# The second attention of a two-layer trunk: scores of a unit adjacent in three PSUM banks under one masked minimum, queries and keys transposed unsplit, norms of two tiles at once

## The chip, the cores and the metric

One core of a Trainium2 chip runs the whole program. The time is the device's, in microseconds (us), from one launch; the figure compared is the median of three runs. On the core, TensorE (PE in the profile, its weight loads PEld) multiplies and transposes, VectorE (DVE), ScalarE (ACT) and GpSimd (POOL) work on tiles, and SyncE (SP) issues the transfers. Each engine executes its own list of instructions in order and waits on semaphores for the others.

## The reference, cut to what matters

The program is a trunk of two layers over 1024 latent tokens of width 1024, with 256 context tokens beside them. Layer 0 has a two-dimensional neighbourhood attention and a gated convolutional feed-forward network; layer 1 has a sliding-window attention and another such network. The change is in the attention of layer 1: 16 query heads of 64 in 4 groups, each group with one key and one value head, a window of 128 to either side, all 256 context keys, and one sink logit per head.

```python
def attn_inputs(h, w_qkv, g_q, g_k, n_kv, with_q=True):
    y = h @ w_qkv
    q = rmsnorm(y[..., :D_MODEL].reshape(bsz, t, n_kv, N_HEADS // n_kv, HEAD_DIM), g_q)
    k = rmsnorm(kv[..., :kv_w].reshape(bsz, t, n_kv, HEAD_DIM), g_k)
...
def attend(q, k, v, bias=None, mask=None, sink=None):
    s = jnp.einsum('...qngd,...knd->...ngqk', q, k).astype(jnp.float32) * (HEAD_DIM ** -0.5)
    s = jnp.where(mask, s, NEG_INF)
    s = jnp.concatenate([s, sink_col], axis=-1)
    p = jax.nn.softmax(s, axis=-1)
    p = p[..., :-1]
...
    def block_step(j):          # 8 blocks of 128 queries
        valid = band & ((kpos >= 0) & (kpos < seq))[None, :]
        mask = jnp.concatenate([valid, ctx_ok], axis=-1)
        return attend(q_j, jnp.concatenate([k_j, k_c], axis=1), jnp.concatenate([v_j, v_c], axis=1),
                      mask=mask, sink=sink)
```

## The kernel before

All arithmetic is in 32 bits. Where a matmul needs the full precision, an operand is kept as two parts in the format that the source calls F32R: a rounded high part ("hi") and the rest ("lo"), and the products of the parts are added in PSUM. A plain F32 tile can be transposed on TensorE as it is.

**Order of the work.** Every stage is planned before it is written out: a scheduler (`Sched`) is given operations with an engine, an estimated cost, a key that says how early each is wanted, what it reads and writes, and which buffers it takes (`acq`) and gives back (`rel`); it lists them engine by engine, and that list is what the engines execute. A table `KINDS` shifts the keys of a kind of operation, a table `RANKS` those of single operations. All instructions are issued by one helper, so that the profile shows them all at line L51; they are told apart by the names of their tiles.

**The stage of the second attention** holds, in one list: the keys and values of the context (`plan_ctx_kv`); 32 tiles of query, key and value (`plan_sw_qkv`: 8 blocks of 128 tokens by 4 groups, each 256 query columns, 64 of key, 64 of value); 64 units of attention (`plan_sw_su` and `plan_su`: a unit is 2 heads of one group for one block of queries); and the output projection (`plan_oproj1`), of which the first half is made inside the stage. Units start behind the tiles that they need (LEAD1 = 7.5 in their keys), so that most of the stage has projection matmuls (`mm`), turns (`pt`), scores (`s`) and products with the values (`pv`) interleaved on PE; when the projection matmuls are used up, matmuls of the output projection (`mm<-o0hi,whi` and its two companions) stand between the last units.

**A tile of query and key** (`plan_sw_qkv`, L2964): ACT copies 384 columns from PSUM (`qraw`); `plan_rstd` (L894) squares 320 of them into `qsq` (ACT), sums per head (DVE, `qv`), takes the power of minus one half on POOL (`qy`) and improves it on DVE by small operations on five columns (one for the mean with epsilon, three of a Newton step); `qn`, `qa`, `qb` and their sum are the scaled and rotated queries and key. ACT then writes the hi parts (`st`, 128x256 for queries and 128x128 for the key, doubled) and POOL or DVE the lo parts (`st`, `klt`). PE turns them: `trk`, one 128x128 transpose of the key's hi and one of its lo, and `trq`, four of the queries' hi and lo side by side. ACT copies the results from PSUM (`kkl`, `kll`, `q`).

**A unit** (`plan_su`, L945): `qkc` makes the context scores of both heads into one bank (four matmuls `s<-ckc,q` of 256 columns), `qkl` the latent scores of each head into a bank of its own (`s<-kkl,q` and `s<-kll,q`, 384 columns, 256 for the first and last block). There are three banks of the tag `s`, taken in turn. For each head DVE copies the context scores to `S` with their sign turned and takes the minimum with the sink (`ctx_part`, `S<-s,sink`); a second pass over the latent scores adds the mask `bandt` and goes on with that minimum (`lat_part`, `S<-s,bandt,m`). Both passes return it through an accumulator, which is read by an instruction of its own. POOL writes the sink's column (`S<-sink`). ACT exponentiates 641 (or 513) columns with that minimum as bias and sums them. PE turns `S` in groups of four 128x128 transposes, two in the last group (`pt<-idr,S`); ACT rounds a group to `pthi`, DVE subtracts for `ptlo`, PE multiplies both with the values (`pv<-pthi,vc`, `pv<-ptlo,vc` for the context, `,v` for latent tokens). Five buffers of `S`, two each of `pthi`, `ptlo` and of the bank tags `pt` and `mm`, one bank `pv`.

`plan_na_qkv`, the same step of the first attention, already takes two tiles at once: one sum over 128x520 and one power over eight columns. It is not part of the change but for the size of three small tiles.

Of the kernel before, what the change touches and what calls it, by code (L numbers as in the profile page):

```python
# [11 lines left out]
F32 = mybir.dt.float32  # L12
F32R = mybir.dt.float32r
AF = mybir.ActivationFunctionType
ALU = mybir.AluOpType
# [23 lines left out]
class InOrder:  # L39
# [7 lines left out]
    def __getattr__(self, name):  # L47
        f = getattr(self.eng, name)

        def call(*a, **k):  # L50
# [16 lines left out]
    sw=dict(cp=0.8, sq=-0.2, red=0.1, newton=-11.7, qn=1.5, qa=4.2, kd=-0.8, ev=9.9, mp=4, v=-2.6, dg=-7.4, bc=9.7,  # L67
          mul=0.4, hif=4.7, lof=0.4, mm=0.2, pw=-0.2, f=-1.5, qb=-0.4, qs=-8.3, qhi=-1.7, trk=-0.9, kev=6.2, lev=-1.5,
          trq=-5.5, qev=0.2, lat_part=-1.4, exp=0.5, lo=-0.2, pvm=0.1, up=-0.4, add=-0.2, rec=-9.6),
# [297 lines left out]
    sw={2: -6.6, 8: -6, 9: -2.2, 13: -4.8, 15: -17.2, 17: -3.9, 24: 6.7, 40: -31.3, 42: 2.4, 50: -2.6, 53: -0.8,  # L367
# [227 lines left out]
def trunk_kernel(ctx, tc, xperm, xtok, xseq, cc, wmod0, wmod, bmod, gnorm, na_wqkv, na_gq, na_gk, na_bias, na_wo,  # L595
# [281 lines left out]
    def plan_qkv_mm(sc, key, psa, h, tt, slabs, s, J, c0=0, hkey=None):  # L877
# [3 lines left out]
        for kt in range(KT):  # L881
            def mm(e, kt=kt):
# [3 lines left out]
                for i, (a, w) in enumerate(((hh, wh), (hl, wh), (hh, wl))):  # L886
# [7 lines left out]
    def plan_rstd(sc, key, J, c0, nh, wk, nsq, fold=None):  # L894

        I = J["id"]

# [15 lines left out]
        def mean(e):  # L913
            v = J["ms"][:, :nh]
            dve.tensor_scalar(out=v, in0=v, scalar1=1.0 / DH, scalar2=EPS, op0=ALU.mult, op1=ALU.add)
# [2454 lines left out]
```

## Time and profile before

| | before |
|---|---|
| median of three runs | 2733.84 us (2731.42 to 2735.31) |
| the profiled execution | 2736.26 us |
| its span (first to last instruction) | 2734.5 us |
| stage of the second attention on PE | 1619.1 to 2047.76 us of the span |
| mean granted TensorE clock | 0.997 of full speed |

The profile is of one execution. Its first part gives the busy time of each engine and its share of the span; then views of the trace give stretches of time (busy time of each engine in each), waits (which engine waited, for whom, in total and how often), groups of equal instructions (busy time, mean of one, idle time of the engine before them and who ended it), and single instructions with their start. Starts and durations of matmuls overlap, since they are pipelined: what one costs PE is the distance to the next start. The stage above runs from the first matmul of the context keys to the first of the output projection's second half.

### The profile page before, as it was taken

Reading aid. Unit: us, or ns where it says so; the run is one execution under the profiler, and the core shown is the slowest. Engines: PE = TensorE matmul, PEld = TensorE weight load, DVE = VectorE, ACT = ScalarE, POOL = GpSimd, SP = SyncE. Lnnn points to the kernel's source line nnn. Section 1 sums busy time; section 2 is a strip of 40 time slices with the busy share of each in tenths; the row PEclk is TensorE's granted clock in tenths of the full one; section 3 lists DMA queues with packets and bytes.
Section 4 is the critical chain, followed back from the end, with each engine's and each line's share of the span. In section 5 each row is a group of like instructions: output and inputs, shape, how many; then the busy total and the mean of one; then the engine's idle time right before and its main releaser. Section 6 shows DMA issues by size and latency. Waiting matters only on the chain.

```text
span 2734.5 us, 43669 instructions
## 1 busy us (share of the span) xinstructions
PE 2700.5 (99%) x15375; PEld 2382.1 (87%) x15375; DVE 2249.7 (82%) x4573; ACT 1665.5 (61%) x3198; POOL 437.2 (16%) x726
## 2 busy tenths in 40 slices
PE   7999999999999999999999999999999999999999
PEld 6999998998799987788888889999988888888887
DVE  5787787789689687899997799888987989888766
ACT  6777676778456554545555458888864655545443
POOL 1222333323000000000010016556430000000000
PEclk9999999999999999999999999999999999999999
DMA  7233333334656644454476561010263234334745
GB/s 288 82 102 105 112 115 101 112 112 141 235 161 186 185 166 135 154 169 135 162 246 220 178 224 33 19 35 19 85 205 123 74 115 154 116 116 144 260 149 190
DMA packets 153104, 387.29 MB, mean 142 GB/s; under 512 B 23356, under 2 KB 38708, under 8 KB 151476
## 3 DMA queue, kind: packets, MB, share of 16 engines
q1 hardware_dynamic: 152884, 384.50, 43.0%
q8 instruction: 121, 1.98, 0.3%
q14 instruction: 99, 0.81, 0.1%
HBM read 313.39 MB, written 71.04 MB: 141 GB/s over the span
## 4 chain that ended last, share of the span: by engine, by line
PE 73%; DVE 2%; ACT 1%; issue 0%; DMA 0%; POOL 0%; SPq 0%; DVEq 0%; ACTq 0%
PE ua L51 17%; PE dn L51 15%; PE uc L51 13%; PE mm L51 7%; PE oacc L51 5%; PE ud L51 4%; PE pt L51 3%; PE pv L51 3%; PE s L51 3%; PE dnc L51 2%; PE u L51 2%; PE mod L51 0%; DVE wlo L51 0%; DVE S L51 0%; DVE o0lo L51 0%
## 5 line engine op out<-in xcount | busy, mean ns | idle before, releaser
L51 ACT ACTIVATE whi<-wraw 128x512 fp32r<-128x512 f32 (+1 forms) x264 | 212.8, 808 | 181.5 <-PE uc L51 53.3
L51 DVE TENSOR_TENSOR wlo<-wraw,whi 128x512 fp32r<-128x512 f32 (+1 forms) x264 | 240.0, 911 | 40.3 <-ACT whi L51 39.9
L51 ACT ACTIVATE S<-S,m 128x640 f32<-128x640 f32 (+3 forms) x288 | 220.6, 767 | 36.7 <-DVE m L51 30.7
L51 ACT ACTIVATE pthi<-pt 128x512 fp32r<-128x512 f32 (+2 forms) x384 | 195.7, 522 | 76.2 <-PE pt L51 37.3
L51 PE MATMUL dn<-ghi,whi 128*128 128x512 f32 x616 | 239.9, 390 | 0.0
L51 PE MATMUL dn<-ghi,wlo 128*128 128x512 f32 x616 | 239.7, 389 | 0.0
L51 PE MATMUL dn<-glo,whi 128*128 128x512 f32 x616 | 239.6, 389 | 0.0
L51 DVE SCALAR_TENSOR_TENSOR u<-c,cv,u 128x1023 f32<-128x1023 f32 x176 | 222.1, 1279 | 3.3 <-ACT u L51 2.8
L51 ACT ACTIVATE whi<-s 128x1024 fp32r<-128x1024 f32 (+1 forms) x116 | 109.1, 940 | 165.0 <-PE uc L51 108.7
L51 ACT ACTIVATE ghi<-graw 128x512 fp32r<-128x512 f32 x154 | 96.4, 630 | 174.6 <-PE dn L51 99.5
L51 PE MATMUL pt<-idr,S 128*128 128x128 f32 x1280 | 194.5, 273 | 1.7 <-DVE pthi L51 1.3
L51 PE MATMUL mm<-whi,h0hi 128*128 128x384 f32 x480 | 168.8, 352 | 0.2 <-ACT qraw L51 0.2
L51 PEld LDWEIGHTS pt<-idr,S 128*128 128x128 f32 x1280 | 152.3, 140 | 16.7 <-DVE pthi L51 3.5
L51 DVE TENSOR_TENSOR glo<-graw,ghi 128x512 fp32r<-128x512 f32 x154 | 105.3, 688 | 71.6 <-ACT ghi L51 65.7
L51 PE MATMUL mm<-wlo,h0hi 128*128 128x384 f32 x480 | 161.5, 336 | 0.0
L51 POOL TENSOR_TENSOR n1y<-n1v,mhalf 128x4 f32<-128x4 f32 (+1 forms) x8 | 9.5, 1182 | 914.9 <-DVE n1v L51 914.9
L51 PE MATMUL pv<-pthi,v 128*128 128x256 f32 (+1 forms) x560 | 151.9, 353 | 3.4 <-DVE pthi L51 3.3
L51 DVE TENSOR_TENSOR pthi<-pt,pthi 128x512 fp32r<-128x512 f32 (+2 forms) x208 | 118.8, 582 | 35.6 <-ACT pthi L51 33.8
L51 DVE TENSOR_TENSOR wlo<-s,whi 128x1024 fp32r<-128x1024 f32 (+1 forms) x116 | 124.3, 1074 | 22.9 <-ACT whi L51 22.6
L51 PEld LDWEIGHTS dn<-ghi,wlo 128*128 128x128 f32 x616 | 115.6, 188 | 24.2
L51 PEld LDWEIGHTS dn<-glo,whi 128*128 128x128 f32 x616 | 115.6, 188 | 23.9
L51 PEld LDWEIGHTS dn<-ghi,whi 128*128 128x128 f32 x616 | 115.6, 188 | 23.7
(410 smaller groups left out, 8642.5 us busy)
## 6 DMA issues: line engine op xcount, KB each, us to landing
wraw<-in_w_up_dram SPq DMA_DIRECT2D x132, 512.0 KB, 3.9
wm<-in_wmod_dram SPq DMA_DIRECT2D x80, 512.0 KB, 4.0
wraw<-in_w_down_dram SPq DMA_DIRECT2D x44, 512.0 KB, 3.6
graw<-g_dram SPq DMA_DIRECT2D x44, 512.0 KB, 4.3
wraw<-in_w_down_dram SPq DMA_DIRECT2D x88, 256.0 KB, 3.1
graw<-g_dram SPq DMA_DIRECT2D x66, 256.0 KB, 2.7
slab<-in_na_wqkv_dram SPq DMA_DIRECT2D x32, 384.0 KB, 4.0
woraw<-in_na_wo_dram SPq DMA_DIRECT2D x24, 512.0 KB, 4.2
```

What stands on the lines that cost most here:

```text
L51: r = f(*a, **k)
```

## The change

Five things change, all in the stage of the second attention.

1. **Scores.** One tile `s3` of 1536 columns (three banks) takes the place of the three rotating banks. The scores of a head lie adjacent in it: the first head has its latent scores in bank 0 and its context scores at the start of bank 1, the second head its context scores at the end of bank 1 or at the start of bank 2. Written out, bank 0 holds the latent scores of one head, bank 1 the context scores of both, bank 2 the latent scores of the other; the middle bank is given back when both heads' minima have read it, the outer ones after one. The scores' matmuls are the same in number and size; they are issued bank by bank.
2. **One masked minimum.** Per head a single pass over 640 columns (512 for the first and last block) adds the mask and takes the minimum, starting from the sink. The mask tile has 7·128 columns, with zeros to either side of the band for the context scores; it lies in this stage's pool, so its load now stands behind the first weight slabs of this stage, and POOL writes the zeros. The sink's column is written first of all into `S`, so POOL now takes the buffer of `S`.
3. **Queries and keys turned unsplit.** The rotated F32 tiles `qa` of two blocks are turned as they are: four transposes for the queries and two for the keys per pair. ACT rounds the turned result from PSUM to the hi parts (`q`, twice 64x512; `kkl`, 128x256), and DVE subtracts for the lo parts (`q`, twice 64x512; `kll`, 128x256). The copies to `st` and `klt` are gone.
4. **Norms of two tiles at once.** Squares of two tiles go into one tile with a column of epsilon per head; one sum of 10 heads, one power of 10 columns, three small operations of 10 columns. The factor of the mean goes into the scale of the gains. The context keys are normed in the same way.
5. **Buffers and tables.** Four buffers of `qraw` for three, four of `qa` for two, a ring of four pairs of `q` for eight tiles; `KINDS` and `RANKS` of the stage are written anew, so that the list is another throughout.

```diff
+    s3 = ps.tile([P, 1536], F32, name="s3", tag="s3", bufs=1)
+    bandt = fin.tile([P, 7 * P], F32, name="bandt")
+    sc = Sched(dict(CAPS, qraw=4, s0=1, s1=1, s2=1, sqs=1, xl=4, qa=4, q=4), {"raw"})
+    sc.op("dma", 1.4, lambda e: dma.dma_start(bandt[:, 2 * P:5 * P], band), writes=[("band",)], key=-205)
...
     sw={2: -6.6, 8: -6, 9: -2.2, 13: -4.8, 15: -17.2, 17: -3.9, 24: 6.7, 40: -31.3, 42: 2.4, 50: -2.6, 53: -0.8,
...
+            for b in sorted(banks):
+                def qkb(e, b=b):
+                    for k, x, w in banks[b]:
...
+                        for i in range(2):
+                            pe.matmul(s3[:, c:c + w], u["q"], u[x][i], start=(i == 0), stop=(i == 1), skip_group_check=True)
+                sc.op("pe", sum(2 * t_pe(w) for _, _, w in banks[b]), qkb, reads=reads, writes=[K("s", b)], key=key,
+                      acq=[(f"s{b}", K("s", b), len({k for k, _, _ in banks[b]}))], rel=[rel] * len(banks[b]))
...
+                    pool.tensor_copy(J["S", k][:, n:n + 1], units[k]["get"]()["sink"])
+                sc.op("pool", 0.13, sink_part, reads=reads, writes=[K("Ss", k)], key=key - 0.5, acq=[("S", K("S", k), uses[k])])
...
-                dve.tensor_scalar(out=J["S", k][:, :TC], in0=J["sc"][:, k * 256:k * 256 + 256], scalar1=-1.0,
-                                  scalar2=u["sink"] if u["sink"] is not None else 3e38, op0=ALU.mult, op1=ALU.min,
-                                  accum_out=J["m", k][:, 0:1])
...
+                    dve.tensor_tensor_reduce(out=J["S", k][:, :n], in0=s3[:, c:c + n], in1=u["mask"], scale=-1.0, scalar=u["sink"],
+                                             op0=ALU.add, op1=ALU.min, accum_out=J["m", k][:, 1:2])
...
+            ahead = j == 0 or (k == 0 and j < 7)
+            at = (1024 if k else 512 - nl) if ahead else (768 if k else 0)
...
-            pe.transpose(J["pt2"][:, 0:P], J["st"][:, 4, :], idr)
-            pe.transpose(J["pt2"][:, P:2 * P], J["klt"].rearrange("p x d -> p (x d)"), idr)
...
+                src = f["a", tt - 1 + i % 2]["a"][:, i // 2 * 2:i // 2 * 2 + 2]
+                pe.transpose(J["pt"][:, i * P:(i + 1) * P], src.rearrange("p h d -> p (h d)"), idf)
...
+                dve.tensor_tensor(out=lo, in0=J["pt"][r, :], in1=hi.bitcast(F32), op=ALU.subtract)
...
+            dve.tensor_tensor(out=kll1[:, cols], in0=J["pt2"][:, :256], in1=kkl1[:, cols].bitcast(F32), op=ALU.subtract)
```

**Turns on PE, in the middle of the stage.** Before, each tile has a pair of transposes for the key (`st` and `klt`) and four for the queries (`st`), between products with the values:

```order
L51 MATMUL pt<-idr,st 128x128
L51 MATMUL pt<-idr,klt 128x128
L51 MATMUL pv<-pthi,vc 128x256 x2
L51 MATMUL pv<-ptlo,vc 128x256 x2
L51 MATMUL pv<-pthi,v 128x256 x2
L51 MATMUL pt<-idr,st 128x128 x4
L51 MATMUL pv<-ptlo,v 128x256 x2
```

In the changed kernel, at the same engine and part of the stage, `qa` is the rotated tile and `s_17895` the three-bank tile:

```order
L51 MATMUL pt<-idr,qa 128x128 x4
L51 MATMUL s_17895<-ckc,q 128x256 x4
L51 MATMUL pv<-pthi,v 128x256
L51 MATMUL mm<-whi,h1hi_17434 128x384
L51 MATMUL mm<-whi,h1lo_17435 128x384
L51 MATMUL mm<-wlo,h1hi_17434 128x384
L51 MATMUL mm<-whi,h1hi_17434 128x384
L51 MATMUL mm<-whi,h1lo_17435 128x384
L51 MATMUL mm<-wlo,h1hi_17434 128x384
L51 MATMUL pt<-idr,qa 128x128 x2
L51 MATMUL pv<-ptlo,v 128x256
```

Six transposes now serve two blocks where six served one; 96 stand in the stage for 192. Matmuls on PE in the stage go from 2956 to 2860, and everything else on PE is the same in number and size.

**Minima on DVE, in the middle of the stage.** Before, each head has two passes (`TENSOR_SCALAR` over the context, `ISA` over the latent scores) with other work between them:

```order
L51 TENSOR_SCALAR S,m_20252<-s,sink 128x256
L51 TENSOR_TENSOR ptlo<-pt,pthi 128x512 x2
L51 ISA S,m_20252<-s,bandt,m_20252 128x384
L51 ISA m_20252 128x1
L51 TENSOR_SCALAR S,m_20293<-s,sink 128x256
L51 TENSOR_REDUCE qv<-qsq 128x5
L51 TENSOR_TENSOR ptlo<-pt,pthi 128x512
L51 ISA S,m_20293<-s,bandt,m_20293 128x384
L51 ISA m_20293 128x1
```

In the changed kernel a piece of the same part, with the lo parts of the queries (`q`) and keys (`kll`) and the small operations of a pair's norm ahead of one head's single minimum:

```order
L51 TENSOR_TENSOR q<-pt,q 64x512 x2
L51 TENSOR_TENSOR osb<-pv,pvup 64x2x128
L51 TENSOR_TENSOR kll_17897<-pt,kkl_17896 128x256
L51 TENSOR_TENSOR v<-qraw,v 128x64
L51 RECIPROCAL rs<-rs 128x32
L51 TENSOR_TENSOR qt<-qy 128x10
L51 TENSOR_TENSOR qt<-qv,qt 128x10
L51 SCALAR_TENSOR_TENSOR qy<-qt,qy 128x10
L51 TENSOR_TENSOR qraw<-qraw,qy 128x320
L51 TENSOR_TENSOR ptlo<-pt,pthi 128x512
L51 ISA S,m_19822<-s_17895,bandt,sink 128x640
L51 ISA m_19822 128x1
```

The two passes are one; the subtraction for queries and keys has come to DVE from POOL, DVE and ACT's copies.

**The end of the stage on PE**, behind the last projection matmul (`mm<-wlo,h1hi`). Before, matmuls of the output projection (`mm<-o0hi`, `mm<-o0lo`) stand between the parts of a unit:

```order
L51 MATMUL pv<-pthi,vc 128x256 x2
L51 MATMUL pv<-ptlo,vc 128x256 x2
L51 MATMUL pv<-pthi,v 128x256 x2
L51 MATMUL pt<-idr,S 128x128 x4
L51 MATMUL pv<-ptlo,v 128x256 x2
L51 MATMUL mm<-o0hi_23774,whi 128x512
L51 MATMUL mm<-o0lo_23776,whi 128x512
L51 MATMUL mm<-o0hi_23774,wlo 128x512
L51 MATMUL pv<-pthi,v 128x256
```

In the changed kernel, some way behind the same point (`rs` is the tile of the sums):

```order
L51 MATMUL pt<-idr,S 128x128 x2
L51 MATMUL pv<-pthi,vc 128x256 x2
L51 MATMUL pv<-ptlo,vc 128x256 x2
L51 MATMUL pv<-pthi,v 128x256 x2
L51 MATMUL pt<-idr,rs 16x128
L51 MATMUL pv<-ptlo,v 128x256 x2
L51 MATMUL pv<-pthi,v 128x256
L51 MATMUL pt<-idr,S 128x128 x4
L51 MATMUL pv<-ptlo,v 128x256
L51 MATMUL pt<-idr,S 128x128 x6
```

Counted from the last projection matmul to the last product with the values, PE has before 106 products `pv`, 98 transposes of `S`, 72 score matmuls and 114 matmuls of the output projection, with 78 of these left behind the last product; after, 126, 118, 86 and 93, with 99 left. Ahead of the stage every engine's list is the same but for the load of the band.

More of the change, by code (lines that the diff above doesn't have):

```diff
@@ L945, in plan_su @@
-    def plan_su(sc, key, I, units, groups, psa, wk, reads, write, sums=None, merge=False):
+    def plan_su(sc, key, I, units, groups, psa, wk, reads, write, sums=None, merge=False, rel=None, s3=None):
         J = {}
@@ L1147, in dg @@
         def dg(e):
-            B["dg"] = wk.tile([P, 672], F32, tag="S", name="S", bufs=SBUFS)
+            B["dg"] = wk.tile([P, SCOL[0]], F32, tag="S", name="S", bufs=SBUFS)
             for i in range(nt):
@@ L1162, in bs @@
         def bs(e):
-            B["bc"] = wk.tile([P, 672], F32, tag="S", name="S", bufs=SBUFS)
+            B["bc"] = wk.tile([P, SCOL[0]], F32, tag="S", name="S", bufs=SBUFS)
             act.activation(B["bc"][:, :n], B["bcp"], AF.Copy)
@@ L2834, in trunk_kernel @@
     ffn(0, op0, None, [0, 1])
-    gqk, sink, bandt, rc, rs = [C1[n] for n in ("gqk", "sink", "bandt", "rc", "rs")]
+    gqk, sink, rc, rs = [C1[n] for n in ("gqk", "sink", "rc", "rs")]
     xs[1] = Parts([lo_part("x1", F32) for _ in range(4)], 2)
@@ L2870, in cp @@
             def cp(e, tt=tt):
[L2871 removed]
+                R[tt] = wk.tile([P, SCOL[0]], F32, tag="S", name="S", bufs=SBUFS)
                 act.activation(R[tt][:, :512], acc[tt], AF.Copy)
@@ L3069, in qev, with red @@
-        def qev(e):
-            q = f["q"][tt] = fin.tile([P, 4, P], F32R, tag="q", name="q", bufs=8)
-            copy(e, q.rearrange("p a b -> p (a b)"), J["pt"].bitcast(F32))
-        sc.op("act", t_actp(512), qev, reads=[K("pt")], writes=[qk], key=key, acq=[("q", qk, 8)], rel=[K("pt")])
+        f["a", tt] = J
+        if tt % 2 == 0:
+            return
+        V = {}
+        def red(e):
+            for x in "vyt":
+                V[x] = tiny.tile([P, 10], F32, tag="q" + x, name="q" + x, bufs=2)
+            dve.tensor_reduce(out=V["v"], in_=sq1, axis=AX.X, op=ALU.add)
@@ new lines, in plan_sw_qkv, with trq @@
+        for T in (tt - 1, tt):
+            chain(f["a", T], T)
+        pr, before = tt // 2, ("q1", g, tt - 1)
+        qk, cols = ("q", g, pr), slice(pr * TC, (pr + 1) * TC)
+        def trq(e):
+            J["pt"] = psa("pt", F32)
+            f["q"][pr] = fin.tile([P, 4, 2 * P], F32R, tag="q", name="q", bufs=4)
+            for i in range(4):
+                src = f["a", tt - 1 + i % 2]["a"][:, i // 2 * 2:i // 2 * 2 + 2]
+                pe.transpose(J["pt"][:, i * P:(i + 1) * P], src.rearrange("p h d -> p (h d)"), idf)
@@ new lines, in plan_sw_qkv, with kh, kl @@
+        for h2, ql in enumerate(late):
+            sc.op("dve", t_dve(512), ql, reads=[K("pt")] + [qk + ("h", y) for y in range(2)], writes=[qk + ("l", h2)], key=key,
+                  rel=[K("pt")], port=False)
+        def kh(e):
+            copy(e, kkl1[:, cols], J["pt2"][:, :256])
+        sc.op("act", t_actp(256), kh, reads=[K("pt2")], writes=[("kk", pr)], key=key, rel=[K("pt2")])
+        def kl(e):
+            dve.tensor_tensor(out=kll1[:, cols], in0=J["pt2"][:, :256], in1=kkl1[:, cols].bitcast(F32), op=ALU.subtract)
@@ L3159, in sums @@
             return RS[g][:, a:a + 1]
-        plan_su(sc, key, I, units, [lst[i:i + 2] for i in range(0, len(lst), 2)], psa, wk, reads, write, sums)
+        plan_su(sc, key, I, units, [lst[i:i + 2] for i in range(0, len(lst), 2)], psa, wk, reads, write, sums, rel=("q", g, j // 2), s3=s3)
         if g < NKV - 1:
@@ L3188, in trunk_kernel @@
         sc.hold("w", ("cw", i), 2)
-    for tag in ("s", "pt"):
-        psa(tag, F32)
+    psa("pt", F32)
     plan_ctx_kv()
```

351 lines of the change are left out of this document (172 added, 179 removed), and 232 rows, old and new, of the table sw.

## The prediction

> **What bounds the kernel now.** I read first the busy times of the whole span, then the stage of the second attention cut into three stretches, then PE's waits there, and last the single matmuls of one stretch. The first line gives each engine's busy time and share:
>
> ```profile
> PE 2700.5 (99%) x15375; PEld 2382.1 (87%) x15375; DVE 2249.7 (82%) x4573; ACT 1665.5 (61%) x3198; POOL 437.2 (16%) x726
> ```
>
> PE is busy 99% of the span. The stretches of the stage (start:end, length, then busy time of PE, PEld, DVE, ACT and POOL with their instructions, TensorE's granted clock, share and rate of the transfers):
>
> ```profile
> 1619.00:1665.00 46.00, 45.86 (x271) 42.82 (x270) 42.67 (x116) 30.77 (x67) 16.33 (x16) 1.00 0.44 149
> 1665.00:1964.00 299.00, 298.74 (x2215) 293.65 (x2214) 260.99 (x869) 254.66 (x647) 169.67 (x378) 1.00 0.11 30
> 1964.00:2048.00 84.00, 80.80 (x487) 70.32 (x486) 75.56 (x177) 60.77 (x125) 34.42 (x46) 1.00 0.64 209
> ```
>
> PE lacks 0.14 us, 0.26 us and 3.20 us of being busy throughout. So in the first two stretches (345 us) PE's own work is the bound, although DVE is busy 87% of the middle one (260.99 of 299) and ACT 85%; only in the last, behind the last projection matmul, do the others make it wait. PE's waits there (in total, times, longest):
>
> ```profile
> PE mm L51 <- DVE o0lo L51: 1.5, 1, 1.5
> PE pv L51 <- DVE osb L51: 1.1, 1, 1.1
> PE pv L51 <- ACT S L51: 0.5, 1, 0.5
> ```
>
> These three make 3.1 of the 3.20 us. The clock is 1.00 in all three stretches, so that a us of work taken off PE's list is a us. What counts is therefore how PE's list shrinks, and whether the last stretch waits more or less. The rest of the program, 2734.5 - 429 = 2305 us, keeps its order but for the load of the band, and I leave it at zero.
>
> **The change part by part. First term: turns on PE.** Matmuls overlap, so their price is the distance between starts. One piece of the middle stretch (start, duration, a group's count at the end):
>
> ```profile
> 1802.16 0.40 PE L51 MATMUL pv<-ptlo,vc 128*128 128x256 f32 x2
> 1802.40 0.34 PE L51 MATMUL mm<-whi,h1hi 128*128 128x384 f32 x1
> ...
> 1804.57 0.28 PE L51 MATMUL pv<-pthi,v 128*128 128x256 f32 x1
> 1804.69 0.22 PE L51 MATMUL pt<-idr,st 128*128 128x128 f32 x1
> ...
> 1804.81 0.35 PE L51 MATMUL pv<-ptlo,v 128*128 128x256 f32 x1
> 1805.00 0.34 PE L51 MATMUL mm<-whi,h1hi 128*128 128x384 f32 x1
> ...
> 1805.52 0.64 PE L51 MATMUL s<-ckc,q 128*128 128x256 f32 x4
> 1805.99 0.34 PE L51 MATMUL s<-kkl,q 128*128 128x384 f32 x1
> 1806.17 0.34 PE L51 MATMUL s<-kll,q 128*128 128x384 f32 x1
> 1806.35 0.47 PE L51 MATMUL pt<-idr,st 128*128 128x128 f32 x4
> 1806.65 0.47 PE L51 MATMUL pv<-pthi,vc 128*128 128x256 f32 x2
> 1806.96 0.60 PE L51 MATMUL pt<-idr,S 128*128 128x128 f32 x4
> 1807.32 0.48 PE L51 MATMUL pv<-ptlo,vc 128*128 128x256 f32 x2
> 1807.63 0.34 PE L51 MATMUL s<-kkl,q 128*128 128x384 f32 x1
> ```
>
> The four `st` take 1806.65 - 1806.35 = 0.30 us, the pair `pv` behind them 0.31 instead of the 0.24 of an undisturbed pair (1802.40 - 1802.16): 0.37 in all. The key's two take 1804.81 - 1804.69 = 0.12, and the single `pv` behind them 0.19 instead of 0.12: 0.19. Unsplit F32 transposes are in the list already, as the turns of `S`: four take 0.36, and 0.31 for the pair behind, 0.43 in all; two are set at half, 0.215.
>
> Removed: 32 tiles × (0.37 + 0.19) = 17.9 us. Added: 16 pairs × (0.43 + 0.215) = 10.3 us. That is -7.6 us. Some of the new groups stand directly ahead of a turn of `S` and so save the step back from transposes to products no second time; about 12 of them at an estimated 0.05 us make 0.6. I take **-7.0 us**. The ends: -7.6 as worked out; and without the 0.07 behind a group (32 × 0.42 - 16 × 0.54) -4.8.
>
> [...] The weight loads of both kinds of turn (the tile turned is the loaded operand) are in the groups of the stage (count, then busy time, mean ns):
>
> ```profile
> L51 PEld LDWEIGHTS pt<-idr,S 128*128 128x128 f32 x608 | 71.7, 140 | 4.5 <-DVE ptlo L51 0.5 <-ACT kkl L51 0.3 <-ACT q L51 0.3
> ...
> L51 PEld LDWEIGHTS pt<-idr,st 128*128 128x128 f32 x176 | 19.9, 140 | 1.9 <-DVE ptlo L51 0.5 <-issue 0.5
> ```
>
> Both have 140 ns, the unsplit `S` and the split `st`, so I add nothing. [...]
>
> **Second term: the other engines, under PE's cover.** The groups of DVE that change or set prices (mean ns behind the busy time):
>
> ```profile
> L51 DVE TENSOR_TENSOR ptlo<-pt,pthi 128x512 fp32r<-128x512 f32 x128 | 85.8, 684 | 12.3 <-ACT pthi L51 10.9 <-PE pv L51 0.4
> ...
> L51 DVE TENSOR_SCALAR_CACHE_REDUCE S<-s,sink 128x256 f32<-128x256 f32 x128 | 59.8, 476 | 6.4 <-PE s L51 4.1 <-PE pt L51 1.9
> L51 DVE CUSTOM_DVE_ANT_0 S<-s,bandt,m 128x384 f32<-128x384 f32 x96 | 57.8, 610 | 2.7 <-PE s L51 1.0
> ...
> L51 DVE CUSTOM_DVE_ANT_0 S<-s,bandt,m 128x256 f32<-128x256 f32 x32 | 14.7, 473 | 1.2 <-PE s L51 0.7
> ...
> L51 DVE DVE_READ_ACCUMULATOR S<-s,sink 128x1 f32 x128 | 10.3, 80 | 0.0
> ```
>
> The minima cost 59.8 + 57.8 + 14.7 + 10.3 = 142.6 us now, without the reading of the second result, which stays. The masked pass costs (610 - 473) / 128 = 1.07 ns a column, so an estimate for 640 columns is 0.610 + 256 × 0.00107 = 0.884, for 512 columns 0.747: 96 × 0.884 + 32 × 0.747 = 108.8 us, or **34 us less on DVE**. New on DVE are the lo parts of the queries, twice per pair at up to 0.684 (the row of 512 columns, though on half the partitions): 32 × 0.684 = 21.9, and of the keys, 16 times at most 0.684: under 11. The norms:
>
> ```profile
> L51 POOL TENSOR_TENSOR qy<-qv,mhalf 128x5 f32<-128x5 f32 x32 | 39.5, 1233 | 33.3 <-DVE qv L51 33.1
> ...
> L51 DVE TENSOR_REDUCE qv<-qsq 128x5 f32<-128x320 f32 x32 | 15.4, 481 | 2.9 <-ACT qsq L51 2.9
> ...
> L51 DVE TENSOR_TENSOR qt<-qy 128x5 f32<-128x5 f32 x32 | 6.4, 200 | 1.6 <-POOL qy L51 1.5
> ```
>
> The sums go from 32 to 16, each longer; of the small operations on columns, four per tile become three per pair: 128 - 48 = 80 fewer at about 0.20 us, 16 us. So DVE's total falls by some 15 to 30 us in 379. ACT loses the copies to `st` and has the same copies out of PSUM in fewer, wider pieces; POOL loses the subtractions for `st` and `klt` and half of the powers. All this lies beside PE where PE lacks 0.40 us in 345, so it can give back no more than that: **0**. If the cover were not there, a pair's norm would be late by about one power, 1.23 us, at the first pair alone; the projection matmuls of the following tiles are queued there. The band's load stands behind the first slabs, and is wanted only when the first unit's scores are there, many tiles later: 0.
>
> One wait is new. POOL now takes `S` for the sink's column ahead of the minimum:
>
> ```profile
> L51 POOL COPY S<-sink 128x1 f32<-128x1 f32 x128 | 23.3, 192 | 12.4 <-PE pt L51 12.4
> ```
>
> The 12.4 us are POOL waiting for PE's turns. Until now DVE waited for the freed `S` itself; now the minimum is later by the copy's 0.192 us where the buffer is the last to come free, and behind it on POOL queue the sums `qa` and the powers. With POOL at 169.67 of 299 us, I put it at 0 in the middle and inside the next term at the end.
>
> **Third term: the end of the stage.** From the lists: behind the last projection matmul stood 106 products with the values and now stand 126, ten to a unit: 10.6 units and 12.6. Between them were 114 matmuls of the output projection and are 93. One such matmul takes an eighth of the distance of these two, eight starts apart:
>
> ```profile
> 2045.95 0.39 PE L51 MATMUL mm<-o0lo,whi 128*128 128x512 f32 x1
> ...
> 2047.76 0.39 PE L51 MATMUL oacc<-o1hi,whi 128*128 128x512 f32 x1
> ```
>
> 1.81 / 8 = 0.226 us. So a unit had 114 / 10.6 × 0.226 = 2.43 us of filling and has 93 / 12.6 × 0.226 = 1.67. A unit's own work on PE: scores 1806.35 - 1805.52 = 0.83 for the context and one head, 0.36 for the other, 2.5 groups of turns 1.08, five pairs of products 1.2: 3.47. ACT's work for one unit comes from these rows:
>
> ```profile
> L51 ACT ACTIVATE S<-S,m 128x641 f32<-128x641 f32 x96 | 79.5, 830 | 5.5 <-DVE m L51 3.9 <-POOL S L51 0.9 <-POOL v L51 0.4
> L51 ACT ACTIVATE pthi<-pt 128x512 fp32r<-128x512 f32 x128 | 74.3, 596 | 15.9 <-PE pt L51 13.7 <-DVE o1lo L51 0.5
> ...
> L51 ACT ACTIVATION_READ_ACCUMULATOR S<-S,m 128x1 f32 x128 | 24.6, 192 | 0.0
> ...
> L51 ACT ACTIVATE pthi<-pt 128x256 fp32r<-128x256 f32 x48 | 18.2, 379 | 8.1 <-PE pt L51 2.4 <-PE pv L51 2.1 <-DVE qn L51 1.5
> ```
>
> 2 × (0.830 + 0.192) + 2 × 0.596 + 0.379 = 3.62 us, before and after. PE with filling exceeded that by 3.47 + 2.43 - 3.62 = 2.28 us, and will by 1.52. DVE's minima and lo parts for a unit fall, by the prices above, from 2 × (0.476 + 0.080 + 0.610) + 2.5 × 0.684 = 4.04 us to 2 × 0.884 + 2.5 × 0.684 = 3.48, so that ACT, not DVE, is the longer, and the margin that shrinks is this one. Waits of 3.20 us over 10.6 units are 0.30 per unit; if they grow as the margin shrinks, 0.30 × 2.28 / 1.52 = 0.45, times 12.6 is 5.7, so **+2.5 us**. That proportion is my choice; the ends are 0.30 × 12.6 - 3.20 = +0.6 with unchanged waits per unit, and 0.60 × 12.6 - 3.20 = +4.4 with twice the waits per unit; if DVE was what mattered (two of the three waits name it), the term falls below nothing, at most -3.20.
>
> Sum: -7.0 + 0 + 2.5 = -4.5 us. The profiled execution took 2736.26 us (span 2734.5 and 1.8 around it), 2.4 us above the median of the runs; I take the sum off the median, 2733.84 - 4.5 = **2729.3 us**.
>
> About 0.2% (5.5 us) is what a measurement of this kernel can tell from no change: faster means below 2728.4, slower above 2739.3.
>
> **The rivals.**
>
> *A, the forecast:* 2729.3, on its own from 2726 (-7.6, waits as now) to 2732 (-4.8, +3). Chance 0.54, of which 0.16 lies below 2728.4.
>
> *B, the end of the stage gains too.* For it: two of the three waits are for DVE, which gets 0.56 us less per unit. Then the 3.20 us go: -7.0 - 3.2 = -10.2, 2723.6; with half of them 2725.2. Against it: there is less filling per unit. Chance 0.24, all faster.
>
> *C, the end eats the gain.* With less filling every second unit waits as long as the longest wait now, 1.5 us: 12.6 / 2 × 1.5 = 9.45, +6.25, sum -0.75: 2733.1, with spread up to 2736. Against it: only three waits in 10.6 units now. That the change does not shorten PE's list would land there as well: if a turn of `qa` cost 1.7 times that of `S`, the first term would be nothing and the sum +2.5, 2736.3. Chance 0.12.
>
> *D, slower: the middle bank.* It holds the contexts of both heads, so the next unit's context scores wait for this unit's second minimum: 0.47 for the four context matmuls and twice 0.884 + 0.080 for the minima and the reading of their results, 2.4 us from their start if DVE is free, and two `ptlo` ahead add 1.37. Before, three banks turned, and the wait was for a bank of the unit before. A unit has about 299 / 53 = 5.6 us in the middle stretch (64 units less the 10.6 at the end), so it holds unless DVE lags by more than some 3 us, but DVE is 87% busy. If a third of the 64 units waits 0.5 us, PE loses 10.7: -4.5 + 10.7 = +6.2, 2740.0. It decides from 10.0 / 64 = 0.16 us a unit. Against it: the scores are issued well ahead, and the order moves other work between. Chance 0.09. [...]
>
> *E, slower: unsplit loads.* If the 96 new loads took twice the 140 ns and none of it were hidden, PE would lose 96 × 0.14 = 13.4: 2742.7. [...] Chance 0.01.
>
> **How the numbers follow.** Faster: 0.16 of A and all of B, 0.40. Same: the rest of A, 0.38, and C, 0.12: 0.50. Slower: D and E, 0.10. The time is A's. The range runs from B's full gain less the spread of the runs (the three runs before lie 1.5 to 2.4 us from their median), 2722, to the upper end of C with that spread, 2737; D, E and a rest of about 0.08 stay out.
>
> **What would show it.** Turns: `pt<-idr,qa` 96 times, four starting 0.36 us ahead of the next, loads of 140 ns; stage on PE 4 to 5 us shorter. Minima: one group of 96 with about 0.88 us, DVE's busy time in the stage down by 15 to 30 us with no gain of its own. The end: PE's idle time behind the last projection matmul 4 to 7 us instead of 3.20; near zero is B, over 9 is C. D would show as PE waiting at `s<-ckc,q` for DVE's minimum in the middle stretch. Wrong altogether would be a change outside the stage of more than 2 us, or PE idle for more than 2 us in its first two stretches.

## The result and the profile after

The changed kernel takes 2752.1 us, median of four runs (2750.84 to 2758.1); the kernel before, run beside it, 2734.57 us (2731.42 to 2735.8). The ratio is 1.007 with a 95% interval of 1.0053 to 1.0088: slower, by about 17 to 18 us, where the prediction had 2729.3 and a range up to 2737. The profiled execution has a span of 2751.4 us. Its busy times over the whole span:

```profile
PE 2703.0 (98%) x15279; PEld 2374.4 (86%) x15279; DVE 2246.3 (82%) x4256; ACT 1647.8 (60%) x3088; POOL 412.8 (15%) x690
```

The shares are within one point of those before; a loss of 0.6% cannot be seen there. The stage must be looked at by itself. From the first matmul of the context keys to the first of the output projection's second half it lasts 448.48 us, before 428.66: +19.8. Up to the last projection matmul it takes 352.69 us (before 344.92), behind it 95.79 (before 83.74). Both parts grew. The same three stretches as before, in the changed kernel (the start, the middle, the end):

```profile
1616.00:1662.00 46.00, 42.79 (x230) 38.20 (x228) 39.27 (x77) 26.98 (x52) 16.95 (x21) 0.96 0.46 159
1662.00:1968.00 306.00, 297.47 (x2100) 286.78 (x2101) 252.75 (x594) 232.28 (x538) 146.39 (x334) 1.00 0.10 28
1968.00:2064.40 96.40, 90.83 (x542) 77.61 (x541) 83.69 (x170) 68.78 (x139) 32.68 (x49) 1.00 0.58 181
```

PE is idle for 3.21 us, 8.53 us and 5.57 us, where it was 0.14, 0.26 and 3.20. The middle stretch, where PE's list was the bound, is the one that changed its nature, although DVE, ACT and POOL are less busy in it than before. PE's waits in the stage (in total, times, longest) say for whom:

```profile
PE s L51 <- DVE m L51: 11.5, 27, 1.1
PE pt L51 <- DVE sq L51: 2.1, 1, 2.1
PE pt L51 <- DVE ptlo L51: 1.6, 3, 1.0
PE mm L51 <- ACT qraw L51: 0.6, 1, 0.6
```

A row that did not exist before leads: score matmuls wait for the result `m` of a minimum, 27 times (8.5 us of it in the middle stretch, 3.0 us at the end). The second row belongs to eight matmuls of one column at the stage's start. They read `sums`, the sums of squares for the norm of the tokens, and in the program they wait for the last addition to `sums`; a `sq` that DVE wrote at the same moment gave the row its name. One of the waits for `m`, among its neighbours on PE and DVE (start, duration; in brackets the idle time and who ended it):

```profile
1706.02 0.42 PE L51 MATMUL s<-kkl,q 128*128 128x384 f32 x1
1706.28 0.34 PE L51 MATMUL s<-kll,q 128*128 128x384 f32 x1
1706.46 0.64 PE L51 MATMUL s<-ckc,q 128*128 128x256 f32 x4
...
1708.53 0.87 DVE L51 CUSTOM_DVE_ANT_0 S<-s,bandt,sink 128x640 f32<-128x640 f32 x1
...
1709.33 0.08 DVE L51 DVE_READ_ACCUMULATOR2_ANT m<- 128x1 f32 x1
1709.33 0.88 DVE L51 CUSTOM_DVE_ANT_0 S<-s,bandt,sink 128x640 f32<-128x640 f32 x1
...
1709.51 0.36 PE L51 MATMUL pv<-pthi,v 128*128 128x256 f32 x1
...
1710.27 0.44 PE L51 MATMUL s<-kkl,q 128*128 128x384 f32 x1 [0.41 <-DVE m L51]
```

The columns decide here. By the diff's `at`, the minimum at 1708.53 belongs to a unit's first head and reads columns 128 to 767 of `s3`: banks 0 and 1. The one at 1709.33 belongs to the second head and reads 768 to 1407: banks 1 and 2. The score matmul at 1710.27 writes columns 128 to 511: bank 0. That bank was free at 1709.40, yet PE waits until the second minimum has ended at 1710.21. The wait is for a minimum that does not read the bank to be written.

All waits of this kind can be told in the same way, by the bank that is written and the banks that the awaited minimum reads. In this trace 32 waits of at least 0.15 us stand ahead of scores. From start to start they are worth 17.7 us; the row of waits shows 11.5, since the ends of matmuls are modelled and hide the first part of each wait. 28 of the 32, worth about 16 us, end about 0.06 us after a minimum that reads other banks; their own bank had mostly been free for 0.7 to 3.3 us. In the built program 104 waits on DVE stand ahead of scores, 97 of them for a minimum, and 38 of these name one that does not read that bank (14 for bank 0, 5 for bank 1, 19 for bank 2). The three counters `s0`, `s1` and `s2` of the scheduler only order its list. The semaphores follow the tile, and `s3` is one tile.

So the theory to be tested was: the waits by tile, on an otherwise better list, are the loss. The rivals: the sums of the tokens' norm, late on DVE beside the first slab's `wlo`, which POOL now makes (the wait of 2.1 us at the stage's start); DVE's new work; and the new list as such.

### The profile page after: what moved, and what is told of

Its sections match the earlier page's. It is cut to its first block, busy times and chain, and to the rows that moved or that the text cites. A ratio compares the mean times of both kernels' runs of the same rounds, so it can differ in the third digit from the quotient of the medians.

```text
span 2751.4 us, 43111 instructions
## 1 busy us (share of the span) xinstructions
PE 2703.0 (98%) x15279; PEld 2374.4 (86%) x15279; DVE 2246.3 (82%) x4256; ACT 1647.8 (60%) x3088; POOL 412.8 (15%) x690
```

## The experiments

The stage's length, first context matmul to first `oacc<-o1hi`, is given with each run, since profiles differ by up to 4 us ahead of the stage.

**The same list with waits by bank.** The change, with each score matmul and each minimum tied to the last users of its own banks, and declared independent of those of other banks. Every engine's list is the same word for word.

```diff
+    def apart(ins, banks, own, other):
+        for b in banks:
+            for o, ob in other[::-1]:
+                if b in ob:
+                    tc.add_manual_dep(ins, o.name, ... reason="same bank")
+                    break
+        for o, ob in other[-48:]:
+            if not (ob & banks):
+                tc.declare_no_dep(ins, o, reason="another bank")
+        own.append((ins, banks))
```

> The changed kernel with its lists word for word, but a score matmul waits only for the minima that read the bank it writes (and a minimum only for the scores in its two banks); in the changed kernel each waits for the last minimum written before it, whichever banks that read. Theory F (waits for minima of other banks): in the trace of the changed kernel 28 of the 32 waits of 0.15 us and more in front of scores end 0.06 us behind a minimum that reads other banks, 17 us in all; they go, and some of it comes back as other waits: 12 to 17 us less, 2735 to 2740 us, PE's waits for `m` at `s` under 3 us instead of 12. Rival R (three banks hold one unit, and the scores wait for their own bank): less than 3 us, the waits stay where they are. Rival L (DVE is late in general): the waits move to the next thing that DVE makes, less than 5 us gained.

Measured: 2732.43 us (2731.43 to 2737.43), ratio to the kernel before 0.9998 (0.9989 to 1.0007); stage 426.78 us. The whole loss is gone, with nothing changed but the waits: 19.7 us, more than the 12 to 17 expected. PE's list is the same in both, so that each start can be compared. Of the 21.7 us by which the stage is shorter, 17.9 stand ahead of scores, 1.2 ahead of the norm's eight small matmuls, about 1.5 between the matmuls right behind these (the last section says why) and 1.0 ahead of turns of `S`. The stretches (start, middle, end):

```profile
1616.40:1662.00 45.60, 44.08 (x251) 40.13 (x250) 41.31 (x84) 29.31 (x59) 18.48 (x26) 1.00 0.45 154
1662.00:1953.00 291.00, 290.85 (x2110) 286.92 (x2109) 252.33 (x595) 231.77 (x538) 146.09 (x334) 1.00 0.12 34
1953.00:2043.20 90.20, 86.60 (x514) 74.06 (x513) 79.34 (x162) 65.53 (x133) 32.47 (x44) 1.00 0.57 184
```

PE lacks 0.15 us in the middle, and at the end 3.60. The waits of the stage:

```profile
PE s L51 <- DVE m L51: 1.6, 4, 0.8
PE pt L51 <- DVE ptlo L51: 1.0, 1, 1.0
PE pt L51 <- DVE sq L51: 0.8, 1, 0.8
```

The leading row has gone from 11.5 us to 1.6, and the four that are left wait for a minimum that reads their own bank.

**The first slab's lo part on DVE instead of POOL**, alone and together with the waits by bank.

```diff
-            ops[i]["fn"](on[i])
+            ops[i]["fn"](getattr(self, "move", {}).get(i, on[i]))
+    sc.move = {next(i for i, o in enumerate(sc.ops) if o["engs"] == list(zip(*WL0))): "dve"}
```

> The changed kernel with one instruction moved: the first slab's lo part of this stage is written by DVE and not by POOL, where it ran beside DVE's sums of squares (seven in 6.70 us against 5.07 in the kernel before). Theory C (POOL and DVE disturb each other there, PE waits 2.06 us for the sums, and the matmuls behind that wait run at twice their distance for some 3 us): the wait falls under 1 us, the slow spell goes, 2 to 4 us less, 2748 to 2750 us. Rival (the sums are late for another reason, the list has PE there too early): 0 to 1 us less.

> Both edits at once. If the two losses are the whole of what went wrong, the first term of the prediction shows: F and C give 15 to 20 us less than the changed kernel, 2732 to 2737 us, about level with the kernel before or a few us below it; with R in place of F not below 2746.

Measured: alone 2751.48 us, ratio 1.0065 (1.0053 to 1.0078), stage 445.62; together 2733.62 us, 1.0002 (0.9993 to 1.0011), stage 428.58. The wait at the stage's start is 1.0 us alone, instead of 2.1, and 1.3 us together; each time is that of its parent within the spread. With the slab left on POOL and the same list the run with waits by bank shows 0.8 us there, so that this wait varies by itself. As the cause of the loss this rival falls.

**The same waits put into the kernel before.** Three banks and two passes as they were; each first score matmul also waits for the last pass of a minimum ahead of it in the program, whichever bank that reads.

```diff
-                pe.matmul(o, u["q"], u["kkc"], start=True, stop=False)
+                r = pe.matmul(o, u["q"], u["kkc"], start=True, stop=False)
+                if I[0] == "su1":
+                    behind(r.ins)
...
+                LASTMIN[0] = dve.tensor_scalar(out=J["S", k][:, :TC], in0=J["sc"][:, k * 256:k * 256 + 256], scalar1=-1.0,
```

> The kernel before with its lists word for word, but each score matmul of the second attention also waits for the last minimum pass written before it, whichever bank that read. Theory F: the same kind of wait costs the kernel before as well, 5 to 18 us (2740 to 2752 us), with waits of PE at `s` for DVE that its trace does not have. Rival R or L: the wait is free where banks are taken in turn and DVE is no later than now: under 2 us.

Measured: 2747.29 us (2745.32 to 2747.61), ratio 1.0049 (1.0037 to 1.0062), stage 442.38: 13.4 us slower by the ratio, with no other part of the change present. Its waits:

```profile
PE s L51 <- DVE m L51: 4.9, 14, 0.8
PE s L51 <- DVE S L51: 1.2, 6, 0.3
```

The row of the changed kernel appears in the old one. The mechanism is enough by itself; it needs neither the new list nor the paired norms.

**The sums of the tokens' norm one step later on PE**, with waits by bank: the eight one-column matmuls over `sums` go behind PE's next operation.

```diff
+            a = order.index(self.later)
+            b = next(x for x in range(a + 1, n) if on[order[x]] == "pe")
+            order.insert(b, order.pop(a))
...
+    sc.later = next(i for i, o in enumerate(sc.ops) if o["fn"].__name__ == "mp")
```

> The kernel of the bank waits (e1) with one step of PE moved: the eight small matmuls that add up the norm's squares stand behind the last six context matmuls, as in the kernel before, and not ahead of them. Theory: the lists of the changed kernel lose at the start of the stage what the turns gain; the wait of 0.8 us in front of these matmuls and the slower matmuls behind it go: 1 to 2.5 us less than e1, 2730 to 2731.5 us. Rival: the wait moves to the matmuls behind them, or differs from run to run by as much: within 1 us of e1.

Measured: 2732.62 us, ratio 0.9996 (0.9988 to 1.0005), stage 426.61, against 2732.43 and 426.78 without the step. The wait ahead of them falls from 0.8 us to 0.5, and nothing is to be had from it.

**One masked minimum taken apart into two passes**, with waits by bank. It is to measure what DVE's saved time is worth under PE's cover. In this edit each pass is tied to both banks of its head, so that a head also holds its two banks for the length of both passes.

```diff
-                    m_ins = dve.tensor_tensor_reduce(out=J["S", k][:, :n], in0=s3[:, c:c + n], in1=u["mask"], ...
+                    apart(dve.tensor_scalar(out=S[:, x:x + TC], in0=s3[:, c + x:c + x + TC], scalar1=-1.0, scalar2=u["sink"], ...
+                    apart(dve.tensor_tensor_reduce(out=S[:, y:y + nl], in0=s3[:, c + y:c + y + nl], in1=u["mask"][:, y:y + nl], ...
```

> The kernel of the bank waits (e1) with each head's minimum taken in two passes, context and then latent, out of the same adjacent scores: DVE gets back the 34 us that the one masked pass saves, everything else in the lists stays. By the prediction's second term (all of it hidden) 0 to 2 us more than e1, 2732 to 2735. Rival: with DVE busy 87% of the middle stretch its time is PE's in the end, and a quarter or more of the 34 us shows: 8 us or more, above 2740.

Measured: 2749.74 us (2747.8 to 2751.59), ratio 1.0058 (1.0045 to 1.007), stage 443.63. The two larger groups of the minima in this run:

```profile
L51 DVE TENSOR_SCALAR_CACHE_REDUCE S<-s,sink 128x256 f32<-128x256 f32 x128 | 61.0, 477 | 6.6 <-PE s L51 4.9 <-PE pv L51 0.8 <-PE pt L51 0.3
L51 DVE CUSTOM_DVE_ANT_0 S<-s,bandt,m 128x384 f32<-128x384 f32 x96 | 59.3, 618 | 3.4
```

The whole stage, first with one pass and waits by bank, then with two passes:

```profile
1616.40:2043.20 426.80, 421.52 (x2871) 401.11 (x2870) 372.97 (x840) 326.60 (x727) 197.04 (x403) 1.00 0.25 79
```

```profile
1617.50:2061.20 443.70, 432.76 (x2871) 399.95 (x2870) 398.77 (x1096) 329.37 (x727) 194.80 (x403) 1.00 0.24 76
```

DVE's load rises by 25.8 us, not by 34, to 90% of the stage (398.77 of 443.70), and the time by about 17 us. So the one pass is worth far more than nothing in this list. PE's waits in the two-pass run begin with

```profile
PE s L51 <- DVE m L51: 4.7, 14, 0.6
```

and start against start 11.7 of the 16.9 us by which the stage is longer stand ahead of scores, 2.8 ahead of turns of `S`. The scores wait for banks that the two passes hold longer. How much of the 17 us is this longer hold, and how much DVE's load as such, this run does not part.

**Without the tables of shifts.** Four kernels with `RANKS` and `KINDS` of this stage left out (one call applies both), so that the lists follow the keys in the code alone: the kernel before; the change with the scores and minima as before (turns and norms only); the change; the change with waits by bank.

```diff
-    sc.rank(RANKS["sw"], KINDS["sw"])
...
     def psa(tag, dt):
-        return s3[:, 0:512] if tag == "s0" else psb(tag, dt)
+        return psb("s" if tag == "s0" else tag, dt)
```

The second pair of lines is in the kernel with turns and norms only, which also takes `plan_su` and the units from the kernel before.

> The kernel before with the tables KINDS and RANKS of this stage left out, so that only the keys in the code order it. With the next three it parts the change from its tables. Expected 5 to 12 us over the kernel before, 2739 to 2746.

> The changed kernel without the tables and without the first two parts of the change: scores in three separate banks taken in turn, two passes per head; turned unsplit, norms of two tiles. By the first term of the prediction 4 to 7 us less than e7; rival (the turns gain nothing, or the pairs come later and make waits): level with e7 or above it.

> The changed kernel without the tables KINDS and RANKS of this stage, its scores waiting as in the changed kernel. Theory F: in another list too the waits for minima of other banks cost 10 us and more against e10. Theory that the changed kernel's own tables were the trouble: level with e10.

> The same without the tables, a score matmul waiting only for the minima that read its bank. Theory F: 10 to 20 us less than e9. Against e8 (turns and norms alone, without tables) it shows what adjacent scores with one pass bring when the waits are right: by e6 (a second pass cost 17 us) 5 to 15 us less than e8, 2737 to 2747; by the prediction's second term level with e8, 2750 to 2754.

| without the tables | us | ratio to before (95%) | stage |
|---|---|---|---|
| before | 2745.08 | 1.0041 (1.0028 to 1.0055) | 438.92 |
| turns and norms only | 2752.02 | 1.0067 (1.0052 to 1.0083) | 445.05 |
| the change | 2766.42 | 1.0122 (1.0107 to 1.0137) | 460.14 |
| the change, waits by bank | 2747.60 | 1.0049 (1.0033 to 1.0066) | 443.12 |

Waits by tile cost 18.8 us in this list too (2766.42 - 2747.60); the loss does not come from the one list that the tables make. The waits on `m` in the change without the tables, and then with waits by bank:

```profile
PE s L51 <- DVE m L51: 9.7, 18, 1.0
```

```profile
PE s L51 <- DVE m L51: 1.0, 3, 0.4
```

The turns and norms alone do not gain in such a list. Up to the last projection matmul they save 8.0 us (343.19 for 351.23), but the end behind it is longer by 14.2 (101.86 for 87.69), and longer waits stand at the start and in the turns:

```profile
PE mm L51 <- DVE n1lo L51: 4.7, 2, 3.4
PE pt L51 <- DVE ptlo L51: 3.2, 5, 2.1
PE pt L51 <- DVE q L51: 2.5, 2, 1.7
```

The granted TensorE clock was also at 0.50 for 13.6 us of this stage (1658.3 to 1665.1 and 1992.8 to 1999.6), and for 6.8 us in the kernel before without the tables. Half of the difference, an estimate, makes up to 3.4 of the 6.1 us between the two stages. In the two runs that part by 18.8 us it was at 0.50 for 10.2 us in both. With the single minimum and waits by bank the time falls by 4.4 us from there, though the intervals of the two ratios overlap. How much of the 14.2 us at the end is less filling and how much is DVE's new work is not separated by these four.

**Each turn twice**, with waits by bank: 96 more transposes of `qa`, into the same places.

```diff
-            for i in range(4):
+            for i in [0, 1, 2, 3] * 2:
...
-            for i in range(2):
+            for i in [0, 1] * 2:
```

> The kernel of the bank waits (e1) with every unsplit turn of a query or key tile made twice, one after the other into the same place: 96 more transposes. By the first term's prices (0.109 us a transpose behind another) and with PE as the bound 96 x 0.109 = 10.5 us more than e1, 2743. Rival (the turns lie where PE waits anyway, so that the first term was worth little): under 5 us more.

Measured: 2741.8 us (2740.92 to 2745.26), ratio 1.0035 (1.0023 to 1.0048), stage 438.17: 9.4 us above the kernel with waits by bank by the medians, 11.4 by the stage. One group in the kernel with waits by bank, single:

```profile
1703.48 0.40 PE L51 MATMUL pv<-ptlo,v 128*128 128x256 f32 x2
1703.72 0.60 PE L51 MATMUL pt<-idr,qa 128*128 128x128 f32 x4
1704.08 0.36 PE L51 MATMUL pv<-pthi,v 128*128 128x256 f32 x1
1704.28 0.34 PE L51 MATMUL s<-kkl,q 128*128 128x384 f32 x1
```

Four take 0.36 us, and the single product behind them 0.20 instead of 0.12. It is the price that the prediction took from the turns of `S`.

**The scaling `qn` on POOL**, with waits by bank: work is taken from DVE below its present load.

```diff
-            ops[i]["fn"](on[i])
+            ops[i]["fn"]("pool" if ops[i]["fn"].__name__ == "qn" and getattr(self, "qn", 0) else on[i])
```

> The kernel of the bank waits (e1) with one kind of operation, the scaling of the 32 query and key tiles by their norms (128x320, 0.52 us on DVE), made by POOL at the same place in the order: about 16 us less on DVE, some 26 more on POOL, an estimate from its 0.81 us for 256 columns. If DVE's time is worth half of itself on PE, as the 17 us for 34 of e6 say: up to 8 us less than e1, 2725 to 2732. Rival (what DVE gains below its present load is hidden, and POOL's longer chain makes the turns later): level with e1 or above it, 2732 to 2745.

Measured: 2733.83 us, ratio 1.0004 (0.9995 to 1.0013), stage 428.42. Its middle stretch:

```profile
1662.00:1953.00 291.00, 290.20 (x2106) 286.57 (x2106) 246.14 (x568) 231.16 (x537) 160.79 (x363) 1.00 0.11 32
```

DVE has 6.2 us less than with waits by bank (252.33), POOL 14.7 more, and PE gains nothing. Over the stage DVE's busy time falls by 6.7 us, not by 16; among others the 54 `qa<-qraw,rc` on DVE now take 25.2 us instead of 21.4. Less work on DVE so shows no gain here. Whether PE covers it, or POOL's slower scaling takes the gain back, this run does not part.

No version is faster than the kernel before; the best, with waits by bank, is level with it.

## Why the prediction was wrong

**The step that failed is the 0 of the second term.** It said of the work on the other engines that "it can give back no more than that: **0**", because PE lacked 0.40 us in the first two stretches. That argument limits a gain only. It says nothing on waits that the change adds to PE's own list in that stretch. "One wait is new", the prediction says, and means the sink's copy; the change added others ahead of scores, 38 for a minimum that does not matter. The waits ahead of scores are worth 17.7 us in the trace, about 16 of it for minima of other banks. With and without the needless ones the medians differ by 19.7 us (2752.1 - 2732.43), in another list by 18.8; put into the kernel before, such waits cost 13.4. The text on the change, and with it the prediction, took the outer banks to be given back after one minimum each; that is what the plan counts, not what the program waits for. The waits of the built list could have been read before any run, and would have shown it.

**Rival D** came nearest: scores that wait for a minimum in the middle stretch, slower, 0.09. It was wrong in its place and reason. It named the context scores of the middle bank, which by the plan comes free only when both minima have read it. The needless waits sit mostly in the outer banks (33 of the 38), at `s<-kkl,q`, for the minimum that does not read them. Its condition, about 0.16 us a unit, was passed: 17.7 / 64 = 0.28.

**The first term, turns, was right.** All groups of turns of queries, keys and `S` with the delay of what follows, waits over 0.06 us taken out, come to 86.4 us before and 79.7 with waits by bank: -6.7, forecast -7.0. The 9.4 to 11.4 us for 96 more transposes fit as well: the prediction's own price for 96 was 16 × 0.645 = 10.3. The weight loads of the unsplit turns and DVE's new groups in the changed kernel:

```profile
L51 DVE CUSTOM_DVE_ANT_0 S<-s,bandt,sink 128x640 f32<-128x640 f32 x96 | 84.0, 879 | 19.9 <-PE s L51 16.9 <-PE pt L51 1.9 <-PE pv L51 0.6
...
L51 DVE CUSTOM_DVE_ANT_0 S<-s,bandt,sink 128x512 f32<-128x512 f32 x32 | 23.6, 745 | 6.5 <-PE s L51 6.1 <-PE pt L51 0.3
L51 DVE TENSOR_TENSOR q<-pt,q 64x512 fp32r<-64x512 f32 x32 | 22.0, 688 | 2.7 <-ACT q L51 1.8
...
L51 PEld LDWEIGHTS pt<-idr,qa 128*128 128x128 f32 x96 | 11.4, 140 | 0.7 <-DVE ptlo L51 0.2
L51 DVE TENSOR_TENSOR kll<-pt,kkl 128x256 fp32r<-128x256 f32 x16 | 6.7, 418 | 2.5 <-ACT kkl L51 2.4
```

The loads of `qa` take 140 ns, like those of the split tiles (176 of `st`, 140 ns, in the kernel before), so rival E is out; no run shows the doubled loads that its 13.4 us were worked out from.

**The prices on DVE were right one by one, their sum was not.** The minima take 0.879 and 0.745 us, estimated at 0.884 and 0.747; the lo parts 22.0 and 6.7 us, against 21.9 and under 11. Yet DVE's busy time fell by only 6.2 us (379.18, from before's whole stage, to 372.97 with waits by bank), not by 15 to 30. The prices are durations, and durations overlap: in the rows of the result the minimum at 1708.53 lasts 0.87 us, the next starts at 1709.33, 0.07 us before its end, and the reading of the result starts together with it. The prediction counted 10.3 us of such readings. DVE has 317 operations fewer (840 for 1157); at 0.07 us each, an estimate from this pair, some 22 us of the durations that went were no busy time of their own. A few operations also came over from POOL, ten `qa` and nine `v` among them. Before's whole stage, for these numbers:

```profile
1619.00:2047.80 428.80, 425.20 (x2968) 406.63 (x2967) 379.18 (x1157) 346.20 (x837) 220.42 (x439) 1.00 0.25 77
```

With `qn` on POOL less work brought nothing; with the two passes more work, and a longer hold of the banks, cost 17 us. "Hidden" can at most have held downwards from the present load.

**The third term.** PE's idle time behind the last projection matmul went from 3.20 to 5.57 us (96.40 - 90.83): +2.4, forecast +2.5, inside the 4 to 7 named. But 3.0 us of it is the waits by tile. With waits by bank it is 3.60, +0.4, just below the lower end of +0.6. The agreement was luck: the number came out for another reason than the filling that it was worked out from.

**What stays open.** With waits by bank the forecast's mechanism is alone, and it gave a stage 1.9 us shorter and no difference in time that could be told, where -7.0 + 0.4 would be -6.6. Some 4.8 us of the turns' gain went again: 1.4 us are in PE's idle time at the start (1.52 for 0.14) and 0.4 at the end; the rest, about 3 us, shows as no idle time of PE, and where it lies was not found.

## What to carry to other kernels

A planner's buffer counters say when it thinks a buffer is free; the waits that the program got here came from its tiles (38 of the 97 for a minimum name one that does not read the bank). Where parts of one tile are given back apart, read the waits of the built list, and make them separate tiles or state the dependences by part. And "hidden under the bound engine" is an upper limit for a gain, never for a loss: ask for each new wait on that engine's own list what is awaited, and price an edit by its stage. Durations that overlap do not add up on the other engines either (here a minimum started 0.07 us before the end of the one ahead): take the distance of starts there too.

## What the runs showed of the hardware

A guard by bank is enough between scores and minima in these runs: in the kernel with waits by bank the `s<-kkl,q` at 1704.28 (shown above) writes bank 0 of `s3` while a minimum from 1703.90 to 1704.78 reads banks 1 and 2. The 19.7 us between the two kernels are the price of guarding by more than that.

TensorE's granted clock fell to 0.55 after a wait of 2.06 us. In the changed kernel PE waits 2.06 us for the sums of the tokens' norm, then has eight matmuls of one column, and from the second on the context matmuls behind stand 0.36 to 0.43 us apart instead of 0.23:

```profile
1625.44 0.39 PE L51 MATMUL mm<-wlo,h1chi 128*128 128x512 f32 x1
1627.89 1.05 PE L51 MATMUL pt<-invd,sums 128*128 128x1 f32 x8 [2.06 <-DVE sq L51]
1628.81 0.48 PE L51 MATMUL mm<-whi,h1chi 128*128 128x512 f32 x1
1629.12 0.56 PE L51 MATMUL mm<-whi,h1clo 128*128 128x512 f32 x1
1629.48 0.63 PE L51 MATMUL mm<-wlo,h1chi 128*128 128x512 f32 x1
1629.90 0.63 PE L51 MATMUL mm<-whi,h1chi 128*128 128x512 f32 x1
```

The granted clock of the 3.6 us from there:

```profile
1628.80:1632.40 3.60, 3.60 (x12) 3.08 (x12) 1.53 (x5) 0.94 (x3) 1.67 (x1) 0.55 0.69 222
```

It is 0.55. From the end of the context matmul ahead (1625.83) to 1628.81 PE had only the wait and eight columns, 3.0 us. With the lower clock behind it the wait costs more than its own 2.06 us: from the first wide matmul behind it to the eleventh after that PE takes 3.90 us here (1628.81 to 1632.71), and 2.35 us in the kernel with waits by bank (1627.82 to 1630.17), where the wait is 0.8 us and the clock stays at 1.00. That is about 1.5 us more. With waits by bank and the slab on DVE a gap of 2.2 us at this place (1624.82 to 1627.06) was also followed by a clock of 0.50, for 3.4 us from 1628.3; gaps of 1.9 us (the slab on DVE alone) and 1.7 us (waits by bank) were not. The gaps of 3.0 and 2.2 us that the lower clock followed hold eight one-column matmuls each; what sets it off beyond that was not shown.
